# Moving the branch to the general path behind the first expert's gate products, with three experts in fixed places instead of two

## The chip, the cores and the metric

The kernel runs on one core of a Trainium2 chip. The metric is the device time of one execution in microseconds, lower is better; the medians below are of several executions. TensorE (PE), VectorE (DVE), ScalarE (ACT), GpSimd (POOL) and SyncE (SP) each work through a queue of their own in order, and wait for each other by semaphores.

## What is computed

Two decoder layers over 512 tokens of width 1024. Layer 0 mixes tokens by retention and a state-space scan, layer 1 by dilated attention; each layer then ends in a mixture of experts: every token goes to two of 16 SwiGLU experts, chosen by a router. Cut to what matters here:

```
logits -> best of 4 groups -> best 2 of its 4 experts, weights by softmax over the two
for each expert e, on the tokens sent to it:
    y = (silu(x @ w_gate[e]) * (x @ w_up[e])) @ w_down[e]      # 1024 -> 512 -> 1024
h = h + sum over the two experts of weight * y
```

A matrix of an expert is 2 MB in float32, so the 16 experts of a layer read 96 MB of weights.

## The kernel before

**The steps of the experts.** The 16 experts run one after the other in places that are heavy (128 rows) or light (64 rows), by the string STEPS = "HHHLHHLHLHHLHHLL". Experts 0 and 1 have fixed places. The other 14 are sorted by load, so that the seven fullest get the heavy places; `by_load` works out the order from the counts of tokens (DVE L1054 to L1058, then a small product on PE, L1060, that gives the list of expert numbers `ids`). If some expert has more rows than the plan holds, a general path (`moe_any`) must run instead. One number, `cmax`, tells this (DVE L1043): every engine loads it into a register (TENSOR_LOAD, L1410) and takes or skips the block (COMPARE_AND_BRANCH, L1411). With the inputs used here the block is skipped. Behind the skip each engine waits for its own earlier work, SP for every DMA it has issued, and the work of other engines from behind the branch waits for DVE to have passed it.

**A heavy step.** A 128-row product runs as three products of rounded parts (`mm3`, L197 to L199): each 128x1024 piece of a weight is split into a rounded part by ACT (CAST, L194) and a rest by DVE (TENSOR_TENSOR, L194), and six products follow for one piece, 24 for a matrix of four pieces. Two rest splits, one in expert 0's w_up and one in expert 1's w_gate, run on POOL. `gate(0)`, `proj(0, "w_up")` (called up(0) below), `gate(1)`, `down(0)` and up(1) follow in this order on PE. `gather(e)` brings an expert's rows into place: for expert 0 by products with a selection (L1249, L1254; one half of them needs token rows that POOL gathered from DRAM, L929), for the others by transposes of rows that `fetch(e)` gathered (POOL L1222). `listed(e)` works out the row numbers for it (PE L1024, L1025, DVE L1012, L1017, L1027). `weights` works out the weight of each row: exponentials on ACT (L1086, with a load of its table before and another after), a chain of small DVE operations (L1088 to L1097), a transpose and a product with the sorted order on PE (L190 on `wt`, L1104).

**The loads.** SP issues the loads of weights in program order, 1 MB each (L1190); where a matrix belongs to a sorted expert, its address needs `ids`, which SP reads by 14 register loads (L1420) behind the branch. F and R are rings of 1 MB buffers; a load waits until the last reader of its buffer is done.

**Order.** A scheduler in the kernel's framework lays each engine's instructions out by priority; `tc.issue_after` adds an order. The branch is a fence: no instruction crosses it.

Of the kernel before, what the change touches and what calls it, by code (L numbers as in the profile page):

```python
# [12 lines left out]
F32R = mybir.dt.float32r  # L13
# [25 lines left out]

STEPS = "HHHLHHLHLHHLHHLL"  # L40
NS = NE - 2
NHEAVY = STEPS[2:].count("H")
# [4 lines left out]
def _constants():  # L47
# [12 lines left out]
    e2 = np.arange(2, 16)  # L60
    th = np.where(e2[None, :] < e_[:, None], -0.5, 0.5)
    heavy, light = iter(range(NHEAVY)), iter(range(NHEAVY, NS))
    rank = [next(heavy) if k == "H" else next(light) for k in STEPS[2:]]
    blk = np.full((128, 4, NS), -1.0)
    for i in range(64):
        if i % 16 >= 2:
            blk[i, i // 16] = rank
    own = (np.arange(16)[None, :] == e_[:, None]).astype(np.float32)
    srt = np.concatenate([blk.reshape(128, 56), own, th], 1).astype(np.float32)
# [26 lines left out]
def kernel(ctx: ExitStack, tc: tile.TileContext, I, out, *_):  # L96
# [686 lines left out]
    def layer1_mix(xT, first):  # L783
# [6 lines left out]
        for hf in range(2):  # L790
# [44 lines left out]
            if hf == 0:  # L835
                params = router_params(1, nc.sync)
# [34 lines left out]
    def router(l, wr, br, wrb):  # L871
# [9 lines left out]
        if l == 0:  # L881
            srts.append(sm.tile([128, 208], F32, bufs=1, name="srt"))
            nc.scalar.dma_start(srts[0][:, 0:86], I["srt"])
# [88 lines left out]
        def chosen_of(c, pl, s0, s1):  # L972
# [9 lines left out]
            for i in range(2):  # L982
                sl = slice(512 * i, 512 * i + 512)

                a, b, o = h[:, c, sl], grow[:, sl], xn[:, sl].rearrange("q (k p) -> q p k", k=4)
                a, b = (t.rearrange("q (p k) -> q p k", k=4) for t in (a, b))
                scaled.append(V.scalar_tensor_tensor(o, a, rs, b, op0=OP.mult, op1=OP.mult))
                nc.scalar.dma_start(xnd[c * 128:(c + 1) * 128, sl], xn[:, sl])
            V.scalar_tensor_tensor(lg[:, c, :], pl, rs, br, op0=OP.mult, op1=OP.add)
            ranks(c)  # L990

        return chunk, q

    def route(q):
# [40 lines left out]
        def loads():  # L1035
# [4 lines left out]
            V.tensor_scalar(m14, pp[:, 4, 2:NE], LIGHT + 0.5, CAP / NHEAVY, op0=OP.is_gt, op1=OP.mult)  # L1040
# [9 lines left out]
        def by_load(bT):  # L1050

            cnt, rank, own, gt = srt[0:64, 116:117], srt[0:64, 117:118], srt[0:64, 86:102], srt[0:64, 120:134]
            P = srt[0:64, 134:190]
            V.tensor_tensor(own, srt[0:64, 56:72], pp[0:64, 4, :], op=OP.mult)  # L1054
            V.tensor_reduce(cnt, own, AX.X, OP.add)
            V.scalar_tensor_tensor(gt, pp[0:64, 4, 2:NE], cnt, srt[0:64, 72:86], op0=OP.subtract, op1=OP.is_gt)
            V.tensor_reduce(rank, gt, AX.X, OP.add)
            V.tensor_scalar(P, srt[0:64, 0:56], rank, None, op0=OP.is_equal)  # L1058
# [6 lines left out]
            V.tensor_copy(pos[:, :, 2:NE], pm)  # L1065
            return P, ids

        def weights(P=None, fits=None):
# [29 lines left out]
            if P is not None:  # L1098
# [6 lines left out]
                V.tensor_copy(wt[:, :, 2:NE], pm)  # L1105
# [67 lines left out]
    def moe(l, rt, norm, done, then=None):  # L1173
# [52 lines left out]
        def gather(e):  # L1226
# [39 lines left out]
        def proj(e, w):  # L1266
# [153 lines left out]
        got, vals = nc.values_load_multi_w_load_instructions(  # L1420
            row[0:1, :], engines=(mybir.EngineType.SP,), min_val=0, max_val=NE - 1,
            skip_runtime_bounds_check_because="sums of one-hot rows: each is one of 2 to 15, or 0")
        ids.update(zip(range(2, NE), vals))
        ids[0] = got[-1]
        listed(2, range(2))
        fetch(2)
        m2r.set([4, 5])
        hs, silu = gate(0)
# [85 lines left out]
```

## Time and profile before

| | us |
|---|---|
| median of 3 runs | 1144.22 (1142.65 to 1145.25) |
| the profiled execution | 1145.4 |
| its span in the trace | 1143.6 |
| PE busy | 1050.0 (92% of the span) |
| DVE busy | 734.0 (64%) |
| ACT busy | 562.2 (49%) |
| POOL busy | 190.1 (17%) |

The profile gives one profiled execution. A busy engine there is not one at its peak; the granted clock of PE is given for stretches of time. "Idle before" names the idle time of an engine just ahead of an instruction and what ended it. Each layer passes the branch once, near 283 us in layer 0 and 833 us in layer 1.

### The profile page before, as it was taken

Reading aid. Unit: us, or ns where it says so; the run is one execution under the profiler, and the core shown is the slowest. Engines: PE = TensorE matmul, PEld = TensorE weight load, DVE = VectorE, ACT = ScalarE, POOL = GpSimd, SP = SyncE. Lnnn points to the kernel's source line nnn. Section 1 sums busy time; section 2 is a strip of 40 time slices with the busy share of each in tenths; the row PEclk is TensorE's granted clock in tenths of the full one; section 3 lists DMA queues with packets and bytes.
Section 4 is the critical chain, followed back from the end, with each engine's and each line's share of the span. In section 5 each row is a group of like instructions: output and inputs, shape, how many; then the busy total and the mean of one; then the engine's idle time right before and its main releaser. Section 6 shows DMA issues by size and latency. Waiting matters only on the chain. (4 is left out here: it accounts for less than half of the span.)

```text
span 1143.6 us, 15992 instructions
## 1 busy us (share of the span) xinstructions
PE 1050.0 (92%) x5951; PEld 762.0 (67%) x5951; DVE 734.0 (64%) x1265; ACT 562.2 (49%) x852; POOL 190.1 (17%) x120
## 2 busy tenths in 40 slices
PE   5979899998799999989889999999978999999994
PEld 4766677786576765757368777877756676565641
DVE  6988952777797755756372273275679785565634
ACT  5433134524576644655353353354366675464634
POOL 3734110000312221221000000000012132211111
PEclk9999999999999999999989999999999999989998
DMA  7262323356699999999842315226349999999963
GB/s 239 74 147 104 101 78 111 107 216 240 240 381 380 380 380 383 373 374 374 309 179 75 110 37 184 74 75 234 141 170 396 354 382 392 388 385 377 367 243 147
DMA packets 84712, 277.38 MB, mean 243 GB/s; under 512 B 23714, under 2 KB 23898, under 8 KB 68368
## 3 DMA queue, kind: packets, MB, share of 16 engines
q1 hardware_dynamic: 72000, 248.31, 57.7%
q0 software_dynamic: 8016, 16.88, 5.9%
q10 hardware_dynamic: 4608, 11.06, 2.6%
q8 instruction: 51, 0.84, 0.3%
q14 instruction: 37, 0.30, 0.1%
HBM read 262.49 MB, written 24.12 MB: 251 GB/s over the span
## 5 line engine op out<-in xcount | busy, mean ns | idle before, releaser
L198 PE MATMUL acc<-R,R 128*128 128x512 f32 x936 | 381.1, 407 | 17.1 <-DVE R L194 16.3
L197 PE MATMUL acc<-R,R 128*128 128x512 f32 x860 | 350.9, 409 | 26.3 <-ACT R L194 16.5
L199 PE MATMUL acc<-R,R 128*128 128x512 f32 x860 | 342.8, 401 | 1.3 <-DVE R L194 1.3
L194 DVE TENSOR_TENSOR R<-F,R 128x1024 fp32r<-128x1024 f32 (+1 forms) x178 | 212.9, 1218 | 138.1 <-ACT R L194 133.1
L194 ACT CAST R<-F 128x1024 fp32r<-128x1024 f32 (+1 forms) x178 | 182.4, 1040 | 180.6 <-PE acc L199 107.7
L198 PEld LDWEIGHTS acc<-R,R 128*128 128x128 f32 x936 | 179.2, 191 | 67.7 <-DVE R L194 28.9
L197 PEld LDWEIGHTS acc<-R,R 128*128 128x128 f32 x860 | 164.2, 191 | 67.7 <-ACT R L194 22.5
L199 PEld LDWEIGHTS acc<-R,R 128*128 128x128 f32 x860 | 164.8, 192 | 37.7 <-DVE R L194 3.3
L1222 POOL DMA_INDIRECT F<-xnd,idx x30 | 50.9, 1698 | 238.7 <-DVE ws L1032 113.9
L1304 PE MATMUL acc<-F,R 128*64 128x512 f32 x304 | 71.2, 595 | 0.0
L194 DVE TENSOR_TENSOR R<-pb,R 128x512 fp32r<-128x512 f32 x84 | 57.3, 702 | 14.6 <-ACT R L194 14.5
L1376 POOL DMA_INDIRECT hd<-m,idx x20 | 36.6, 1829 | 147.8 <-ACT m L1375 146.0
L194 ACT CAST R<-pb 128x512 fp32r<-128x512 f32 x84 | 47.5, 586 | 27.4 <-PE pb L190 20.9
L194 DVE TENSOR_TENSOR R<-R,R 128x1024 fp32r<-128x1024 f32 x40 | 48.2, 1221 | 6.4 <-ACT R L194 6.0
L922 POOL MEMSET R<- 128x1024 f32 x2 | 1.9, 954 | 300.6 <-PE acc L199 300.6
L1304 PEld LDWEIGHTS acc<-F,R 128*64 128x64 f32 x304 | 22.0, 137 | 43.6 <-issue 43.2
L194 ACT CAST R<-R 128x1024 fp32r<-128x1024 f32 x40 | 41.4, 1050 | 13.2 <-PE acc L199 12.1
L197 PE MATMUL acc<-spare,R 128*128 128x512 f32 x116 | 45.7, 394 | 0.0
L199 PE MATMUL acc<-spare,R 128*128 128x512 f32 x116 | 45.7, 394 | 0.0
L190 PE MATMUL pb<-C,F 128*128 128x128 f32 (+1 forms) x296 | 37.5, 261 | 3.4 <-POOL F L490 3.4
L190 PE MATMUL pb<-C,m 128*128 128x128 f32 (+1 forms) x163 | 27.7, 292 | 12.7 <-DVE m L227 9.6
L1307 ACT ACTIVATE m2w<-acc 64x512 f32<-64x512 f32 x8 | 4.7, 593 | 68.5 <-PE acc L1304 68.5
(384 smaller groups left out, 1447.0 us busy)
## 6 DMA issues: line engine op xcount, KB each, us to landing
F<-in_moe_w_up_dram SPq DMA_DIRECT2D x46, 1024.0 KB, 22.4
F<-in_moe_w_down_dram SPq DMA_DIRECT2D x40, 1024.0 KB, 22.2
F<-in_moe_w_gate_dram SPq DMA_DIRECT2D x38, 1024.0 KB, 23.0
R<-in_moe_w_gate_dram SPq DMA_DIRECT2D x20, 1024.0 KB, 15.9
R<-in_moe_w_down_dram SPq DMA_DIRECT2D x12, 1024.0 KB, 24.9
h<-in_moe_w_down_dram SPq DMA_DIRECT2D x12, 1024.0 KB, 22.5
F<-in_c_w_qkv_dram SPq DMA_DIRECT2D x12, 1024.0 KB, 6.1
F<-in_ab_w_in_dram SPq DMA_DIRECT2D x10, 1024.0 KB, 5.1
```

Of the source, the lines that this page charges most:

```text
L190: PE.transpose(dst, src, ident[:n, :n])
L194: return S.copy(hi, src), eng.tensor_tensor(lo, src, hi.bitcast(F32), op=OP.subtract)
L197: PE.matmul(ps, ah, bh, start=first, stop=False)
L198: PE.matmul(ps, ah, bl, start=False, stop=False)
L199: return PE.matmul(ps, al, bh, start=False, stop=last)
L922: G.memset(q.x0, 0.0)
L1222: rows[e] = G.indirect_dma_start(out=xg[e % 2][0:n], out_offset=None, in_=xnd[:, :], in_offset=bass.IndirectOffsetOnAxis(ap=idx[0:n, e, 0: ...
L1304: m = PE.matmul(ps[LIGHT * i:LIGHT * i + LIGHT], x_[:, 4 * kk + k, :], raw[i][:, k, :], start=kk + k == 0, stop=kk + k == 4, skip_group_ch ...
L1307: silu = S.activation(hs[0:LIGHT], ps[LIGHT:2 * LIGHT], AF.Silu)
L1376: G.indirect_dma_start(out=hd[:, :], out_offset=bass.IndirectOffsetOnAxis(ap=idx[:, e, 1:2], axis=0), in_=y[:, :], in_offset=None, bounds_ ...
```

## The change

- FIXED = 3: experts 0, 1 and 2 have fixed places and 13 are sorted. The loads of expert 2's w_gate and of expert 1's w_down, 4 MB, stand ahead of the branch on SP, expert 2's w_up directly behind it, ahead of the register loads of `ids`.
- `by_load` and `gate(0)` stand ahead of the branch; so do three rest splits of up(0) (two on DVE, one on POOL). `listed` and `fetch` of experts 1 and 2 stand behind it. Expert 0's splits are ordered behind the sort's last DVE step.
- The router's parameters of layer 1 are loaded from layer 1's first mixing stage, no longer ahead of layer 0's branch. In the last 128 tokens of the router the logits and ranks stand ahead of the scaled rows.

The core of the diff (sizes of the table of the sort follow from 14 to 13 and are left out):

```diff
+FIXED = 3
-NS = NE - 2
-NHEAVY = STEPS[2:].count("H")
+NS = NE - FIXED
+NHEAVY = STEPS[FIXED:].count("H")
...
-                params = router_params(1, nc.sync)
+                with tc.issue_after(fr.load.ins):
+                    params = router_params(1, nc.sync)
...
+            if c < 3:
+                rows()
             V.scalar_tensor_tensor(lg[:, c, :], pl, rs, br, op0=OP.mult, op1=OP.add)
             ranks(c)
+            if c == 3:
+                rows()
...
-            V.tensor_scalar(P, srt[0:64, 0:56], rank, None, op0=OP.is_equal)
+            by_load.last = V.tensor_scalar(P, srt[0:64, 0:4 * NS], rank, None, op0=OP.is_equal)
...
-            if e < 2:
+            if e < FIXED:
                 return wv[w][e, r0:r1, :].rearrange(f"{rows} n -> p k n", p=128)
...
-            with tc.issue_after(ids[0].ins) if (e, w) == (1, "w_down") else nullcontext():
-                fr.load = nc.sync.dma_start(t, rows_of(e, w, r0, r1))
+            fr.load = nc.sync.dma_start(t, rows_of(e, w, r0, r1))
...
-                with after(loads.last.ins) if e == 0 else nullcontext():
+                with after(by_load.last.ins) if e == 0 else nullcontext():
...
-                    for i in (rt.last, rt.sqrt) + (gather.last if k2 else ()) if held else ():
+                    for i in (rt.last, rt.sqrt, by_load.last) + (gather.last if k2 else ()) if held else ():
...
         cf, bT = loads()
+        perm, row = by_load(bT)
         gather(0)
+        table(AF.Silu)
+        R[wrs[2]] = typed(wrs[2:], F32R)[0]
+        m2r.set([4, 5])
+        hs, silu = gate(0)
         top = nc.values_load(cmax[0:1, 0:1], min_val=0, max_val=T)
+        m2r.set([0, 1])
+        m4r.set([0, 1])
         with tc.If(top > CAP):
             moe_any(l, weights(), xg[1])
-        table(AF.Silu)
+        m2r.set([5, 4])
         m4r.set([1])
-        R[wrs[2]] = typed(wrs[2:], F32R)[0]
-        perm, row = by_load(bT)
         listed(1, range(2))
         fetch(1)
         listed(0, range(2), rt.oh)
-        got, vals = nc.values_load_multi_w_load_instructions(
+        _, vals = nc.values_load_multi_w_load_instructions(
...
         listed(2, range(2))
         fetch(2)
-        m2r.set([4, 5])
-        hs, silu = gate(0)
```

The line numbers in the rows of the changed kernel are some 4 to 15 higher than before (L194 becomes L198, L197 to L199 become L201 to L203). In the rows of the order R_, F_ and m_ are buffers with their numbers.

On DVE in layer 0, about the branch, before: R_84, R_85 are expert 0's w_gate pieces, R_82 its rows.

```order
L194 TENSOR_TENSOR R_84<-R_2390,R_84 128x1024
L1043 CAST cmax<-cf 128x1
L194 TENSOR_TENSOR R_82<-acc,R_82 128x512 x2
L1056 SCALAR_TENSOR_TENSOR srt<-pb,srt 64x14
L194 TENSOR_TENSOR R_85<-R_2390,R_85 128x1024
L1410 TENSOR_LOAD cmax
L1411 COMPARE_AND_BRANCH
```

The same place in the changed kernel; R_2390 and R_2391 hold w_gate, F_70 the first half of w_up.

```order
L198 TENSOR_TENSOR R_84<-R_2390,R_84 128x1024
L198 TENSOR_TENSOR R_85<-R_2390,R_85 128x1024
L198 TENSOR_TENSOR R_2444<-R_2391,R_2444 128x1024
L1443 TENSOR_SCALAR cf<-cf 128x1
L198 TENSOR_TENSOR R_84<-R_2391,R_84 128x1024
L198 TENSOR_TENSOR R_85<-F_70,R_85 128x1024
L198 TENSOR_TENSOR R_2444<-F_70,R_2444 128x1024
L1425 TENSOR_LOAD cmax
L1428 COMPARE_AND_BRANCH
```

All four rest splits of gate(0) and two of up(0) now precede DVE's branch; before, two of gate(0) did and the sort was cut in two by it.

On PE in layer 0, the end of up(0) before; `wt` is the table of the rows' weights, F_79 the rows that were fetched for expert 1, `spare` the rounded part whose rest POOL splits.

```order
L197 MATMUL acc<-R_84,R_82 128x512
L198 MATMUL acc<-R_84,R_82 128x512
L190 MATMUL pb<-C,wt 64x128
L199 MATMUL acc<-R_84,R_82 128x512
L197 MATMUL acc<-spare_2874,R_82 128x512
L198 MATMUL acc<-R_2873,R_82 128x512
L199 MATMUL acc<-spare_2874,R_82 128x512
L197 MATMUL acc<-spare_2874,R_82 128x512
L1104 MATMUL pb<-srt,m_1_91 128x56
L190 MATMUL pb<-C,F_79 128x128 x8
```

The same place in the changed kernel:

```order
L201 MATMUL acc<-spare_2872,R_82 128x512
L202 MATMUL acc<-R_2871,R_82 128x512
L203 MATMUL acc<-spare_2872,R_82 128x512
L201 MATMUL acc<-spare_2872,R_82 128x512
L202 MATMUL acc<-R_2871,R_82 128x512
L203 MATMUL acc<-spare_2872,R_82 128x512
L194 MATMUL pb<-C,wt 64x128
L1115 MATMUL pb<-srt,m_1_91 128x52
L194 MATMUL pb<-C,F_79 128x128 x8
```

The transpose of `wt` stood within up(0), with seven of its products still behind it (five are in the rows, two stand behind expert 1's transposes), and now stands behind up(0)'s last product.

On SP in layer 0 the loads that led up to the branch in the changed kernel (before, the row of F_76 was the last of the weights here):

```order
L1200 DMA F_77<-in_moe_w_down_dram 128x2x1024
L1200 DMA F_76<-in_moe_w_up_dram 128x2048
L1200 DMA R_2389<-in_moe_w_down_dram 128x2x1024
L1200 DMA R_2387<-in_moe_w_gate_dram 128x2048
L1200 DMA R_2388<-in_moe_w_down_dram 128x2x1024
L1425 TENSOR_LOAD cmax
L1425 ISA x2
L1428 COMPARE_AND_BRANCH
```

R_2389, R_2387, R_2388 are loads that stood behind the branch and behind `ids`; F_78, likewise, now stands earlier still.

## Rows read from the trace of the kernel before

**Rows 1.** PE's timeline (start, us, engine, line, operation, tiles, idle before) in both layers

```profile
288.08 0.77 PE L197 MATMUL acc<-R,R 128*128 128x512 f32 x1 [4.58 <-DVE srt L1058]
...
312.85 0.50 PE L198 MATMUL acc<-R,R 128*128 128x512 f32 x1 [2.32 <-DVE R L194]
...
316.85 0.50 PE L197 MATMUL acc<-R,R 128*128 128x512 f32 x1 [0.73 <-ACT R L194]
...
830.36 2.05 PE L1254 MATMUL acc<-m,F 128*128 128x128 f32 x16
836.90 0.47 PE L197 MATMUL acc<-R,R 128*128 128x512 f32 x1 [4.50 <-DVE srt L1058]
...
848.71 0.50 PE L198 MATMUL acc<-R,R 128*128 128x512 f32 x1 [2.62 <-DVE R L194]
...
855.91 0.39 PE L197 MATMUL acc<-R,R 128*128 128x512 f32 x1
856.14 0.40 PE L198 MATMUL acc<-R,R 128*128 128x512 f32 x1
...
861.65 0.80 PE L198 MATMUL acc<-R,R 128*128 128x512 f32 x1 [2.35 <-DVE R L194]
...
862.67 0.63 PE L197 MATMUL acc<-R,R 128*128 128x512 f32 x1
863.10 0.63 PE L198 MATMUL acc<-R,R 128*128 128x512 f32 x1
...
867.12 0.50 PE L197 MATMUL acc<-R,R 128*128 128x512 f32 x1 [0.72 <-ACT R L194]
```

**Rows 2.** Sequencer records of the branch, line L1411, both layers (ns min/median/max)

```profile
L1411 PEldq COMPARE_BRANCH  x2: 3328/3378/3427, 284.4 to 833.2; - x2
```

**Rows 3.** DVE's timeline in layer 1

```profile
831.43 1.21 DVE L194 TENSOR_TENSOR R<-R,R 128x1024 fp32r<-128x1024 f32 x1
...
832.63 1.27 DVE L194 TENSOR_TENSOR R<-acc,R 128x512 fp32r<-128x512 f32 x2
...
842.56 0.68 DVE L1012 TENSOR_TENSOR m2w<-C,pos 128x512 bf16<-128x512 f32 x1
...
844.50 2.90 DVE L1017 TENSOR_TENSOR junk<-C,pos 128x512 bf16<-128x512 f32 x1
...
850.92 0.16 DVE L1088 TENSOR_REDUCE gv<-gd 128x4 f32<-128x16 f32 x1
...
852.13 0.23 DVE L1097 TENSOR_TENSOR wt<-wt,m 128x64 f32<-128x64 f32 x1
```

**Rows 4.** POOL's timeline in layer 1

```profile
844.47 2.38 POOL L194 TENSOR_TENSOR R<-F,spare 128x1024 fp32r<-128x1024 f32 x1 [0.29 <-DVE idx L1027]
```

**Rows 5.** ACT's timeline in layer 1

```profile
845.97 0.60 ACT L1297 ACTIVATE m<-acc 128x512 f32<-128x512 f32 x1 [0.62 <-PE acc L199]
846.46 1.04 ACT L194 CAST R<-F 128x1024 fp32r<-128x1024 f32 x1
847.51 1.28 ACT L1086 ACT_TABLE_LOAD   x1
```

**Rows 6.** Windows of layer 1: busy time by engine, granted clock, DMA share, GB/s

```profile
845.00:850.00 5.00, 2.38 (x11) 1.64 (x10) 5.00 (x6) 4.33 (x6) 3.13 (x2) 1.00 0.87 314
...
860.00:870.00 10.00, 7.62 (x28) 6.02 (x29) 7.74 (x9) 3.96 (x6) 2.25 (x2) 0.83 1.02 388
```

**Rows 7.** ACT's waits, 318 to 572 us (us in total, times, longest)

```profile
ACT R L194 <- DMA F<-in_moe_w_up_dram: 0.9, 1, 0.9
```

**Rows 8.** POOL's timeline in layer 0, first token rows gathered

```profile
270.60 1.80 POOL L929 DMA_INDIRECT R<-xnd,idx  x1 [29.37 <-DVE rs L219]
```

**Rows 9.** Landing times of the gathers of line L929

```profile
DMA to landing us min/median/max: 4.2/4.7/5.1
```

**Rows 10.** PE's timeline in layer 0 about that gather

```profile
273.20 0.40 PE L199 MATMUL acc<-R,R 128*128 128x512 f32 x1
...
276.96 2.03 PE L1249 MATMUL acc<-C,R 128*128 128x128 f32 x16
```

More of the change, by code (lines that the diff above doesn't have):

```diff
@@ L59, in _constants @@
     e_ = p % 16
-    e2 = np.arange(2, 16)
+    e2 = np.arange(FIXED, NE)
     th = np.where(e2[None, :] < e_[:, None], -0.5, 0.5)
     heavy, light = iter(range(NHEAVY)), iter(range(NHEAVY, NS))
-    rank = [next(heavy) if k == "H" else next(light) for k in STEPS[2:]]
+    rank = [next(heavy) if k == "H" else next(light) for k in STEPS[FIXED:]]
     blk = np.full((128, 4, NS), -1.0)
     for i in range(64):
-        if i % 16 >= 2:
+        if i % 16 >= FIXED:
             blk[i, i // 16] = rank
     own = (np.arange(16)[None, :] == e_[:, None]).astype(np.float32)
-    srt = np.concatenate([blk.reshape(128, 56), own, th], 1).astype(np.float32)
+    srt = np.concatenate([blk.reshape(128, 4 * NS), own, th], 1).astype(np.float32)
     cst[:, C_EC] = e_
@@ L882, in router @@
             srts.append(sm.tile([128, 208], F32, bufs=1, name="srt"))
-            nc.scalar.dma_start(srts[0][:, 0:86], I["srt"])
+            nc.scalar.dma_start(srts[0][:, 0:S_TAB], I["srt"])
         q.srt = srts[0]
@@ L981, in chosen_of, with rows @@
                 q.xn.append(xn)
[L982 to L988, printed above, removed]
+            def rows():
+                for i in range(2):
+                    sl = slice(512 * i, 512 * i + 512)
+                    a, b, o = h[:, c, sl], grow[:, sl], xn[:, sl].rearrange("q (k p) -> q p k", k=4)
+                    a, b = (t.rearrange("q (p k) -> q p k", k=4) for t in (a, b))
+                    scaled.append(V.scalar_tensor_tensor(o, a, rs, b, op0=OP.mult, op1=OP.mult))
+                    nc.scalar.dma_start(xnd[c * 128:(c + 1) * 128, sl], xn[:, sl])
+            if c < 3:
+                rows()
             V.scalar_tensor_tensor(lg[:, c, :], pl, rs, br, op0=OP.mult, op1=OP.add)
             ranks(c)
+            if c == 3:
+                rows()
         return chunk, q
@@ L1050, in by_load @@
         def by_load(bT):
-            cnt, rank, own, gt = srt[0:64, 116:117], srt[0:64, 117:118], srt[0:64, 86:102], srt[0:64, 120:134]
-            P = srt[0:64, 134:190]
-            V.tensor_tensor(own, srt[0:64, 56:72], pp[0:64, 4, :], op=OP.mult)
+            cnt, rank, own, gt = srt[0:64, 116:117], srt[0:64, 117:118], srt[0:64, 86:102], srt[0:64, 120:120 + NS]
+            P = srt[0:64, 134:134 + 4 * NS]
+            V.tensor_tensor(own, srt[0:64, S_OWN:S_TH], pp[0:64, 4, :], op=OP.mult)
             V.tensor_reduce(cnt, own, AX.X, OP.add)
-            V.scalar_tensor_tensor(gt, pp[0:64, 4, 2:NE], cnt, srt[0:64, 72:86], op0=OP.subtract, op1=OP.is_gt)
+            V.scalar_tensor_tensor(gt, pp[0:64, 4, FIXED:NE], cnt, srt[0:64, S_TH:S_TAB], op0=OP.subtract, op1=OP.is_gt)
             V.tensor_reduce(rank, gt, AX.X, OP.add)
-            V.tensor_scalar(P, srt[0:64, 0:56], rank, None, op0=OP.is_equal)
+            by_load.last = V.tensor_scalar(P, srt[0:64, 0:4 * NS], rank, None, op0=OP.is_equal)
             pi = bank(shape=(1, NS))
@@ L1064, in by_load @@
             PE.matmul(pm.rearrange("p c s -> p (c s)"), bT, P, start=True, stop=True)
-            V.tensor_copy(pos[:, :, 2:NE], pm)
+            V.tensor_copy(pos[:, :, FIXED:NE], pm)
             return P, ids
@@ L1419, in moe @@
         listed(0, range(2), rt.oh)
-        got, vals = nc.values_load_multi_w_load_instructions(
+        _, vals = nc.values_load_multi_w_load_instructions(
             row[0:1, :], engines=(mybir.EngineType.SP,), min_val=0, max_val=NE - 1,
-            skip_runtime_bounds_check_because="sums of one-hot rows: each is one of 2 to 15, or 0")
-        ids.update(zip(range(2, NE), vals))
-        ids[0] = got[-1]
+            skip_runtime_bounds_check_because="sums of one-hot rows: each is one of FIXED to 15, or 0")
+        ids.update(zip(range(FIXED, NE), vals))
         listed(2, range(2))
         fetch(2)
-        m2r.set([4, 5])
-        hs, silu = gate(0)
         fr.set([[0, 2, 3, 4, 7, 5, 6, 1, 8, 12, 13, 14, 10, 11], [1, 3, 4, 2, 6, 0, 7, 5, 8, 12, 13, 14, 10, 11]][l])
```

5 lines of the change are left out of this document (3 added, 2 removed).

## The prediction

> **What bounds the kernel now.** I read first the busy time of the engines: PE 92% of the span, no other above 64%. So what counts is where PE stands still, and the timeline of PE with its idle times shows that next. At the change's place it stands still three times in each layer [rows 1]: 4.50 us (4.58 in layer 0) from the end of expert 0's gather to the first gate product, 2.62 us at the start of up(0), 2.35 us (2.32) in the middle of gate(1). The reader is to see the releaser of each: the first is put down to DVE's sort (L1058), the others to a rest split. Then the records of the branch itself: on PE's sequencer the jump over the block takes 3.33 and 3.43 us [rows 2]. So the first gap has two causes of nearly one length, the jump and DVE's queue (rest splits and sort), which run side by side. The two other gaps come from POOL: its split takes 2.38 us from 844.47 [rows 4], and a DVE operation that starts 0.03 us later takes 2.90 us [rows 3], where the operation of the same size ahead of it took 0.68. DVE does next to nothing while POOL splits.
>
> That is how the trace shows it, and the page "Trainium Architecture — The Big Picture" of the Trainium skill, section "What this means for kernel authors", gives the rule: DVE and GpSimd contend for one port pair, and it is an exclusive lock, not a split of bandwidth. The trace agrees, with 2.90 beside 2.38 us. Were it a split, a POOL split beside DVE would cost about half, and each sum below would be some 1.2 us lower per layer.
>
> Last the windows: from 845 to 850 the DMA engines are 87% busy [rows 6], and PE waits for no load; ACT waits for one load in all of layer 0's expert steps, 0.9 us [rows 7].
>
> **The change part by part.** Times are those of layer 1 in the profiled execution. The four parts are gate(0), the branch, the weights and gate(1); then the loads.
>
> *Gate(0) ahead of the branch.* Expert 0's gather ends on PE at 830.36 + 2.05 = 832.41 [rows 1]. In the new order of DVE, an operation of 0.68 us that waits for this end, and the sort's last step (0.24, an estimate by its class: it is smaller), come first: 833.35. Then two splits of the rows (1.27 for both) and some 0.3 of small casts: 834.95. Rest splits follow at 1.21 each [rows 3]: 836.2, 837.4, 838.6. The fourth reuses the buffer of the first, so it needs the first's six products (6 x 0.23 = 1.4, by the distance of 855.91 and 856.14 [rows 1]), then an ACT cast of 1.04 [rows 5]: 838.65, so 839.9. Its six products end at 841.3. Before, the gate's end was read by ACT at 845.97 [rows 5]: 4.7 us gained.
>
> *The branch behind it.* PE's jump costs its 3.4 us wherever it stands, and at its new place PE has nothing to run beside it: 841.3 + 0.3 for the register + 3.4 = 845.0. DVE comes to the same time: POOL's split starts when the fourth rest split is done, 839.9, and holds DVE until 842.3; two rest splits of up(0) make it 844.7, and PE's first work behind the branch waits for DVE to have passed. So of 4.7 us about 3.7 come back as a new idle time between gate(0) and up(0). In exchange the 2.62 us at 848.71 are gone, since POOL's split and its two followers lie under the jump. After some 24 small products of `listed` (0.7 us, an estimate from their start distances), up(0) begins at 845.8 and runs 24 x 0.23 = 5.6 us, to 851.4. Were the jump to go, PE would still wait for DVE's 844.7; only with both away does the gain stay.
>
> *The weights behind up(0).* ACT now has two casts that wait for up(0)'s own products (1.04 each, the second can start at 848.7 and ends at 849.8), then the load of the exponentials' table, 1.28, and the exponentials: 851.3. On DVE the product with up(0)'s result is ahead of the rest of the chain, then nine small operations, 850.92 to 852.36 or 1.4 us [rows 3]: 853.6. PE, which had the transpose of `wt` within up(0), now has nothing between 851.4 and 853.6: a new wait of 2.2 us. Its cover before was seven products of up(0); that is gone.
>
> *Gate(1).* The product with the sort's order and the transposes of expert 1's rows take about 1.6 us: 855.2. POOL's second split starts about then, as soon as ACT has cast its input, and DVE cannot split expert 1's rows before 857.7; with 0.64 us for a first half gate(1) starts at 858.4 and runs 5.6 us, to 864.0. The 2.35 us gap in it is gone, since the wait now lies ahead of it. By the distance from the last row at half speed to 867.12, down(0) starts 1.4 us later: 865.4, 1.7 us before the row's 867.12 [rows 1]. Layer 0 had 316.85 - 288.08 = 28.8 us from restart to down(0), layer 1 30.2 [rows 1]; what differs is the half-speed stretch at 861.65. So in layer 0 the same sum gives only 0.3 us. Both: -2.0.
>
> *The clock.* After the idle 4.50 us PE runs at half speed, in both layers; after 2.35 us it did in layer 1 and did not in layer 0 (0.63 us long rows, 0.43 apart, against 0.50 at 312.85 [rows 1]; granted clock 0.83 over 860 to 870 [rows 6]). At half speed PE has 1.2 of its 2.4 GHz. A mean of 0.83 over 10 us is 3.4 us at half; that holds 8 products at 0.43 instead of 0.23, so it costs 1.6 us where PE sets the pace. Before, the first stretch lay in gate(0), where splits set much of the pace. Now the idle times are 2.5 us ahead of gate(0), 3.7 ahead of up(0), and 2.2 and 2.9 ahead of gate(1). Nothing of this length but 4.50 and 2.35 is in the rows, so the bounds are no stretch (0) and two on the path in each layer (+6.4); 3.7 lies nearer to 4.50, so I take one in each layer: +3.1, rounded with its partial overlap of `listed`.
>
> *The loads.* 4 MB of weights go out ahead of the branch, and 2 MB more before SP reads `ids`. In layer 1 the DMA engines are nearly idle there, and nothing on the path waits for them: 0. In layer 0 two of these loads find their buffers free only when products up to 273.20 + 0.40 have read them [rows 10], while the gather of expert 0's rows (issued at 270.60 [rows 8], 4.2 to 5.1 us to land [rows 9], so 275.7) is in flight; its reader starts at 276.96 [rows 10], 1.2 us of room. If the last 2.1 us of the gather run at half rate it lands at 277.8: +0.9, which I take. If it had to wait for both megabytes at 388 GB/s (2.1 MB, 5.4 us), it would land at 279 or later: about +2. If nothing is shared: 0. Behind the branch the stream of loads is some 11 us ahead (4 x 1.05 MB at 388 GB/s); there is one wait for a load of 0.9 us to win [rows 7], of which I take 0.6.
>
> *The rest at nothing.* The parameters of layer 1's router move on SP alone, and are a few kilobytes each. The logits ahead of the rows for the last tokens move DVE's work under products of L1249 and L1254, which PE runs ahead of the counts anyway. One sorted place fewer shortens DVE operations of 0.2 us by nothing that shows.
>
> **Sum:** -2.0 + 3.1 + 0.9 - 0.6 = +1.4 us on 1145.4. The profiled execution is 1.2 us above the median, so 1145.7 against 1144.22.
>
> **The rivals.**
>
> *The gain at up(0) is kept.* up(0) starts 2.6 to 2.9 us earlier in each layer. For it to last, the weights' chain would have to be hidden (if ACT's casts come sooner than I have them) and no half-speed stretch fall on the path. Then -2.6 twice, and -1.4 for layer 1's stretch at 861.65: 1138 or so; with only the second, -2.0 - 0.6 = 1141.6. Middle: 1140. For it speaks that 2.35 and 2.62 us left the clock alone in two of the rows; against it that PE's program has the transpose of `wt` behind all of up(0).
>
> *The jump goes.* If PE's sequencer gets past the branch while PE still works on queued products, and DVE with it, 3.4 us more per layer go: about 1136. Against it: the jump took 3.3 to 3.4 us both times [rows 2], and DVE is not there before 844.7.
>
> *Slower: the clock.* More pauses in place of one long one mean more stretches at half speed, and now on up(0) and gate(1), whose 5.6 us are all PE's. With two in each layer: -2.0 + 6.4 + 0.9 - 0.6 = +4.7, and up to +1 more from the gather: 1149 to 1150.2. It decides from the third of the four stretches on (-1.7 + 3 x 1.6 = +3.1, over the bound). For it speaks the row at 861.65, where 2.35 us were enough; against it 312.85.
>
> **How the numbers follow.** A measurement of this kernel tells about 0.2%, 2.3 us, from no change: 1141.9 to 1146.5 is the same. My forecast, 1145.7 (1143 to 1148), has a chance of 0.42 (0.03 faster, 0.33 same, 0.06 slower); the gain kept, 0.26 (0.22 faster, 0.04 same); the jump gone, 0.05, faster; the clock, 0.27 (0.24 slower, 0.03 same). So faster 0.30, same 0.40, slower 0.30. The range from 1139 to 1150.5 leaves out the jump's case, the far end of the kept gain and the far end of the clock's.
>
> **What would show it.** Right: PE's gap ahead of gate(0) down to 2 to 3 us, a new one of 3 to 4 us ahead of up(0) that ends with DVE or with PE's own sequencer, one of about 2 us ahead of the transpose of `wt`, one ahead of gate(1) that ends with a rest split beside POOL's; down(0) 28 to 30 us behind the first product's old place. Wrong: PE's branch record well under 3 us; no gap ahead of `wt`; in layer 0 the products of L1249 more than 1 us late, with an idle time ahead of them that ends with a DMA. The forecast falls if stretches at half speed number none or four, or if a part far from the branch moves by more than a microsecond.

## The result, and the profile after

| | before | after |
|---|---|---|
| median, us | 1143.45 (1142.65 to 1145.25, 4 runs) | 1132.81 (1130.76 to 1133.92, 4 runs) |
| ratio, 95% interval | | 0.9903 (0.9881 to 0.9924) |
| span of the profiled execution, us | 1143.6 | 1132.1 |

The change is 1% faster, some 11 us. The prediction said 1145.7 with a range from 1139: it was 13 us too high, and the time lies below its range.

At the branch the trace shows much of what was predicted. PE's timeline of the changed kernel, first layer 0, then layer 1 (the rows answer to those of [rows 1]):

```profile
285.87 0.50 PE L202 MATMUL acc<-R,R 128*128 128x512 f32 x1 [2.03 <-DVE R L198]
294.50 0.18 PE L1035 MATMUL pb<-tl,junk 128*128 128x2 bf16 x1 [3.05 <-DVEq L1428]
304.04 0.30 PE L194 MATMUL pb<-C,wt 128*64 128x128 f32 x1 [1.80 <-DVE wt L1108]
...
831.76 0.50 PE L202 MATMUL acc<-R,R 128*128 128x512 f32 x1 [2.03 <-DVE R L198]
840.37 0.18 PE L1035 MATMUL pb<-tl,junk 128*128 128x2 bf16 x1 [3.06 <-DVEq L1428]
842.56 0.16 PE L1036 MATMUL pb<-rc,m2w 128*128 128x2 bf16 x1 [1.55 <-issue]
852.63 0.30 PE L194 MATMUL pb<-C,wt 128*64 128x128 f32 x1 [1.92 <-DVE wt L1108]
853.28 0.42 PE L1115 MATMUL pb<-srt,m 64*128 64x52 f32 x2 [0.35 <-ACT m L1113]
857.39 0.79 PE L203 MATMUL acc<-R,R 128*128 128x512 f32 x1 [1.18 <-DVE R L198]
```

The gap of 4.5 us ahead of gate(0) is down to 2.0. A new one of 3.1 us stands behind gate(0) and ends with DVE's sequencer at the branch. The weights' chain, hidden before, now holds PE for 1.9 + 0.35 us, and a rest split that stands behind POOL's second one (854.26 to 856.62 us) holds gate(1). All four were steps of the prediction. So the gain must have come from elsewhere.

Three views show where. First the costliest groups of the page (line, operation, shapes, count, busy us, mean ns, idle before and its releaser), before and then after. They are the first two products of `mm3`, L197 and L198 before; the third, L199, waits for 1.3 us before:

```profile
L198 PE MATMUL acc<-R,R 128*128 128x512 f32 x936 | 381.1, 407 | 17.1 <-DVE R L194 16.3
L197 PE MATMUL acc<-R,R 128*128 128x512 f32 x860 | 350.9, 409 | 26.3 <-ACT R L194 16.5
```

```profile
L202 PE MATMUL acc<-R,R 128*128 128x512 f32 x936 | 378.0, 404 | 6.5 <-DVE R L198 6.5
L201 PE MATMUL acc<-R,R 128*128 128x512 f32 x860 | 351.8, 410 | 7.6 <-ACT R L198 6.6
```

PE's idle time ahead of them is down from 43.4 to 14.1 us. That is far more than the gaps at the branch hold.

Second, the distance between the light gates, which are blocks of 32 products that stand in the same order in every kernel. The start of each block in PE's timeline (before: 428.72, 484.39, 539.15; after: 428.84, 478.10, 529.01) gives:

| start of light gate to the next, us | before, layer 0 | after, layer 0 | before, layer 1 | after, layer 1 |
|---|---|---|---|---|
| expert 3 to 6 | 49.2 | 49.2 | 49.0 | 49.0 |
| 6 to 8 | 30.7 | 31.0 | 30.5 | 30.9 |
| 8 to 11 | 55.7 | 49.3 | 57.1 | 49.0 |
| 11 to 14 | 54.8 | 50.9 | 56.2 | 50.9 |

The gain lies in the two late stretches: 10.3 us in layer 0 and 13.4 in layer 1, 23.7 together, more than 100 us behind the branch. What the changed kernel loses elsewhere brings this down to 11.

Third, what PE waited for in the first of these stretches before. PE's timeline, then ACT's:

```profile
438.08 0.50 PE L197 MATMUL acc<-R,R 128*128 128x512 f32 x1 [0.63 <-ACT R L194]
439.03 0.50 PE L197 MATMUL acc<-R,R 128*128 128x512 f32 x1 [0.44 <-ACT R L194]
...
457.95 0.50 PE L197 MATMUL acc<-R,R 128*128 128x512 f32 x1 [1.55 <-ACT R L194]
459.21 0.80 PE L198 MATMUL acc<-R,R 128*128 128x512 f32 x1 [0.76 <-DVE R L194]
```

```profile
435.88 0.59 ACT L1307 ACTIVATE m2w<-acc 64x512 f32<-64x512 f32 x1 [12.10 <-PE acc L1304]
436.50 0.58 ACT L194 CAST R<-pb 128x512 fp32r<-128x512 f32 x1
436.98 1.05 ACT L194 CAST R<-F 128x1024 fp32r<-128x1024 f32 x1
```

ACT stands idle for 12.1 us until the light gate of expert 8 is done, for its silu (L1307) is next in its queue; the casts of w_down of expert 7 come behind it, and PE then waits for them. The same four waits come again at 493.75 to 514.74, and in layer 1. They are 3.4 of the 6.4 us by which the first stretch of layer 0 is longer than in the changed kernel. The rest is slower products behind them, part of it at half speed (the granted clock over the stretch is 0.97, and 1.00 in the changed kernel). After, ACT has these casts ahead of the silu, with the loads just in time:

```profile
428.46 1.05 ACT L198 CAST R<-F 128x1024 fp32r<-128x1024 f32 x1 [1.22 <-DMA F<-in_moe_w_down_dram]
429.41 1.04 ACT L198 CAST spare<-F 128x1024 fp32r<-128x1024 f32 x1
436.00 0.59 ACT L1317 ACTIVATE m2w<-acc 64x512 f32<-64x512 f32 x1 [5.55 <-PE acc L1314]
```

Two things have changed there at once. The scheduler has put the casts ahead of the silu; and the loads are in fact earlier. The experiments are to tell these apart, and to price the branch by itself. (One correction to what stands ahead: the branch is not a fence for everything. Loads that depend on nothing behind it are issued ahead of it, and so the early loads are possible.)

### The profile page after: what moved, and what is told of

Its sections match the earlier page's. It is cut to its first block, busy times and chain, and to the rows that moved or that the text cites. A ratio compares the mean times of both kernels' runs of the same rounds, so it can differ in the third digit from the quotient of the medians.

```text
span 1132.1 us, 15979 instructions
## 1 busy us (share of the span) xinstructions
PE 1051.2 (93%) x5951; PEld 769.5 (68%) x5951; DVE 731.5 (65%) x1265; ACT 569.7 (50%) x856; POOL 187.2 (17%) x120
## 5 line engine op out<-in xcount | busy, mean ns | idle before, releaser
L201 PE MATMUL acc<-R,R 128*128 128x512 f32 x860 | 351.8, 410 | 7.6 <-ACT R L198 6.6
L203 PE MATMUL acc<-R,R 128*128 128x512 f32 x860 | 342.3, 401 | 3.5 <-DVE R L198 3.5
L198 DVE TENSOR_TENSOR R<-F,R 128x1024 fp32r<-128x1024 f32 (+1 forms) x178 | 217.0, 1236 | 166.7 <-ACT R L198 161.1
L198 ACT CAST R<-F 128x1024 fp32r<-128x1024 f32 (+1 forms) x178 | 182.5, 1040 | 208.1 <-PE acc L203 117.3
L201 PEld LDWEIGHTS acc<-R,R 128*128 128x128 f32 x860 | 164.8, 192 | 51.5 <-ACT R L198 12.7
L203 PEld LDWEIGHTS acc<-R,R 128*128 128x128 f32 x860 | 165.0, 192 | 42.1 <-DVE R L198 6.0
L1232 POOL DMA_INDIRECT F<-xnd,idx x30 | 48.0, 1600 | 226.8 <-DVE ws L1043 151.0
L198 DVE TENSOR_TENSOR R<-pb,R 128x512 fp32r<-128x512 f32 x84 | 56.5, 686 | 13.1 <-ACT R L198 12.7
L198 ACT CAST R<-pb 128x512 fp32r<-128x512 f32 x84 | 47.8, 587 | 30.1 <-PE pb L194 24.4
L198 DVE TENSOR_TENSOR R<-R,R 128x1024 fp32r<-128x1024 f32 x40 | 47.6, 1220 | 6.9 <-ACT R L198 6.7
L198 ACT CAST R<-R 128x1024 fp32r<-128x1024 f32 x40 | 41.5, 1050 | 12.5 <-PE acc L203 12.3
L203 PE MATMUL acc<-spare,R 128*128 128x512 f32 x116 | 45.6, 393 | 0.0
L201 PE MATMUL acc<-spare,R 128*128 128x512 f32 x116 | 45.4, 392 | 0.0
L194 PE MATMUL pb<-C,F 128*128 128x128 f32 (+1 forms) x296 | 41.2, 274 | 3.4 <-POOL F L494 3.4
L194 PE MATMUL pb<-C,m 128*128 128x128 f32 (+1 forms) x163 | 26.5, 285 | 17.2 <-DVE m L231 14.2
L194 PEld LDWEIGHTS pb<-C,m 128*128 128x128 f32 (+1 forms) x163 | 19.4, 146 | 30.2 <-issue 11.6
```

The source lines that it names most:

```text
L194: PE.transpose(dst, src, ident[:n, :n])
L198: return S.copy(hi, src), eng.tensor_tensor(lo, src, hi.bitcast(F32), op=OP.subtract)
L201: PE.matmul(ps, ah, bh, start=first, stop=False)
L203: return PE.matmul(ps, al, bh, start=False, stop=last)
L1232: rows[e] = G.indirect_dma_start(out=xg[e % 2][0:n], out_offset=None, in_=xnd[:, :], in_offset=bass.IndirectOffsetOnAxis(ap=idx[0:n, e, 0: ...
```

## The experiments

Ratios are to the kernel before, on the same chip; one percent is 11.4 us. The kernel before has medians from 1143.5 to 1148.8 us on the chips used, so kernels are compared by ratio. Where times of stretches are given "by the starts of like instructions", they come from one profiled execution each.

| run | edit | ratio (95% interval) | light gates 8 to 11, 11 to 14, layer 0 | layer 1 |
|---|---|---|---|---|
| before | | 1 | 55.7, 54.8 | 57.1, 56.2 |
| after | | 0.9903 (0.9881 to 0.9924) | 49.3, 50.9 | 49.0, 50.9 |
| e1 | branch at its old place | 0.9829 (0.9793 to 0.9865) | 49.3, 50.6 | 49.0, 50.4 |
| e2 | changed kernel with two fixed | 1.0046 (1.0025 to 1.0067) | 49.5, 57.6 | 49.3, 58.2 |
| e3 | before, other order alone | 0.9919 (0.9893 to 0.9945) | 52.1, 52.1 | 52.0, 52.3 |
| e4 | 4 MB copied behind the branch | 0.9988 (0.9965 to 1.0012) | 49.3, 51.0 | 49.0, 50.8 |
| e5 | table load held | 0.9877 (0.9847 to 0.9908) | 49.3, 50.5 | 49.0, 50.5 |
| e6 | e1, no split on POOL | 0.9789 (0.9756 to 0.9822) | 49.3, 50.5 | 49.0, 50.5 |
| e7 | e1, two gathers held | 0.9824 (0.9795 to 0.9853) | 50.2, 49.9 | 50.1, 49.8 |
| e8 | before, three fixed and early loads alone | 0.9816 (0.9787 to 0.9845) | 49.3, 50.5 | 49.1, 50.4 |
| e9 | before, fast order forced, no lead | 0.9924 (0.9897 to 0.9951) | 50.8, 53.0 | 50.6, 56.4 |
| e10 | e8, old order forced, lead kept | 0.9838 (0.9812 to 0.9864) | 51.0, 51.0 | 50.9, 50.8 |
| e11 | e8, loads held | 0.9964 (0.9946 to 0.9982) | 55.9, 54.8 | 55.8, 56.0 |
| e12 | e8, no split on POOL | 0.9758 (0.9734 to 0.9782) | 49.3, 50.5 | 49.0, 50.5 |

Some results fit none of what was expected: e2 (1151.3 us) is slower than both of its theories, and the medians of e3 (1137.7), e5 (1131.3) and e10 (1128.8) lie between the ranges of two theories.

### The two halves of the change: e1, e2 and e8

e1 is the changed kernel with `by_load`, `gate(0)` and the rest of the tail where the kernel before has them.

```diff
-        perm, row = by_load(bT)
         gather(0)
-        table(AF.Silu)
...
-        hs, silu = gate(0)
         top = nc.values_load(cmax[0:1, 0:1], min_val=0, max_val=T)
...
         with tc.If(top > CAP):
             moe_any(l, weights(), xg[1])
...
+        table(AF.Silu)
...
+        perm, row = by_load(bT)
...
+        hs, silu = gate(0)
```

> The changed kernel with its branch, sort and gate(0) back at the old place; three fixed experts, the early loads, the router's parameters and the order of the last rows stay. Theory O: the gain comes late in the experts' steps (about -10 us in layer 0 from 420 to 530 us, -13 in layer 1 from 970 to 1075), where a new order of PE closes waits of 0.6 + 0.4 + 1.6 + 0.8 us in two places per layer; the order there is that of the changed kernel, so this gain stays, and the +1.1 and +2.3 us that the new branch cost at the start of the steps are gone: 1126 to 1131. Theory S: the gain comes from the branch behind the gate products: 1142 to 1145.

e2 is the changed kernel with its branch behind gate(0), but two fixed experts, so that none of expert 2's loads can go ahead. Expert 1's w_down, 2 MB, still goes ahead of the branch (SP issues it from 263.63 us).

```diff
-FIXED = 3
+FIXED = 2
```

> The changed kernel with FIXED = 2: 14 experts are sorted, expert 2's 4 MB cannot be loaded ahead of the branch; branch, sort and gate(0) stay moved. Theory O: of the two places in each layer whose waits closed, the first keeps the new order and the second has the old one again, so about half of the late gain is lost (4 to 6 us per layer): 1139 to 1144. Theory S: 1132 to 1134, as the branch is still moved.

e8 is e1 without the edits of the router's parameters and rows: the kernel before with three fixed experts and their loads, and nothing else.

```diff
-                with tc.issue_after(fr.load.ins):
-                    params = router_params(1, nc.sync)
+                params = router_params(1, nc.sync)
...
-            if c < 3:
-                rows()
+            rows()
```

> The kernel before with three fixed experts and their early loads alone: the router's parameters and the last rows stand where they stood before. The order on PE, row for row, is that of e1_branch_early. If these two edits are worth nothing: as e1, 1124 to 1128. If not, the difference is theirs.

The third fixed expert with its early loads gains 1.84% (21 us). e1 and e8 differ by less than their intervals, so the smaller edits are worth nothing that shows. In the changed kernel the moved branch takes part of the 21 back: e1 stands 0.74% (8.5 us) ahead of it. e2, 0.46% (5 us) slower than the kernel before, is no price of the move alone. By the starts of like instructions it gains 9.2 us in the late stretches (its row in the table) and loses 5.6 us at the branch of layer 0, 6.6 at that of layer 1 and 4.1 in layer 1's mixing; PE's jump, 6.4 us in it, and the mixing are taken up below.

### Order or lead: e3, e7, e9, e10, e11

e3 leaves loads and branch as before and calls `gather(e + 2)` ahead of `down(e)` for experts 8 and 11.

```diff
-            if e + 1 < NE:
+            if e + 1 < NE and e not in (9, 12):
                 gather(e + 1)
...
+            if e in (8, 11):
+                gather(e + 2)
```

> The kernel before, with one edit: for the steps 8 and 11 (light ones between two heavy ones) the rows of the expert after next are gathered ahead of the light step's down products, not behind. Loads, branch and sort as before. Theory O with order alone: the waits of 1.55 + 0.76 us and the half-speed stretch after one of them in each layer go at both places, about 2.3 to 4 us each, 1130 to 1135. Theory L (the lead of the loads is what pays, or is needed): the loads are no earlier than before, and in the kernel before some of them land only a few us ahead of their use, so PE waits for loads instead: 1140 to 1144.

e7 is e1 with the transposes of experts 10 and 13 held behind the light steps' down products, close to their old place.

```diff
+                        with after(pe[-1].ins) if e in (10, 13) else nullcontext():
+                            tr(pts[i][:, a, :], x_[:, blk])
```

> The kernel of e1_branch_early, with the order of the kernel before put back at one kind of place: the rows for experts 10 and 13 are transposed behind the down products of the light steps 8 and 11, two places per layer; loads and their lead as in e1. Theory O (the order pays): the waits of 1.55 + 0.76 us come back at each place, and where the clock falls some 1.6 us more, 9 to 16 us in all: 1134 to 1141. Theory L (the lead pays): 1125 to 1128.

e3 gains 0.8% by order alone, so order can matter; e7 shows that these two gathers are not what it hangs on. What differs between the queues is ACT's: the casts ahead of the silu or behind it. So the last set forces just that. e9 is the kernel before with the order of the fast kernels: in `down(7)` and `down(10)` the casts (four and two) come first, then the silu of the light gate, then the rest, and the transposes of gather(9) and gather(12) stand behind the down products.

```diff
+            ahead = [wsplit(raw[i // 2][:, :, i % 2 * 512:i % 2 * 512 + 512]) for i in range({7: 4, 10: 2}.get(e, 0))]
+            with ExitStack() as st:
+                if ahead:
+                    with after(wsplit.hi.ins):
+                        st.enter_context(after(silu().ins))
+                evac = split_to(hh, hl, pt)
...
+                        with after(pe[-1].ins) if e in (9, 12) else nullcontext():
+                            tr(pts[i][:, a, :], x_[:, blk])
```

> The kernel before, with two fixed experts and its loads as they were, but with the order of the fast kernels forced at two places of each layer: ScalarE casts w_down of experts 7 and 10 (four and two tiles) ahead of the silu of the light step that follows, instead of behind it, and the transposes of gather(9) and gather(12) stand behind the down products of experts 7 and 10. Theory order (the early loads only made the scheduler choose this order, and the order is the whole gain): 1122 to 1127 us, and the waits of PE on ScalarE's casts near 438, 458, 494 and 513 us are gone. Theory lead (4 MB loaded ahead of the branch are the gain, since the DMA engines are full from 350 us to the end of the layer): 1141 to 1146, the casts now wait for their loads instead. If both are needed: 1130 to 1139.

e10 is e8 with the opposite: the casts of `down(7)` and `down(10)` held behind that silu, the loads early.

```diff
-                        for i in evac if k2 >= 1 and e >= 8 else ():
+                        for i in (evac if k2 >= 1 and e >= 8 else ()) + ((silu,) if e in (7, 10) else ()):
```

> Experiment e8 (three fixed experts and their early loads alone, 1124.5) with ScalarE's casts of w_down of experts 7 and 10 held behind the silu of the light step that follows, as they stand in the kernel before; the loads keep their lead. Theory order: 1140 to 1146, with PE's waits on ScalarE's casts back, some 5 us at each of four places. Theory lead: 1122 to 1127. If both are needed: 1130 to 1139.

e11 is e8 with the early loads held until SP has read `ids`, as before.

```diff
+            with tc.issue_after(ids[0].ins) if (e, w) in ((1, "w_down"), (2, "w_gate")) else nullcontext():
+                fr.load = nc.sync.dma_start(t, rows_of(e, w, r0, r1))
...
+                with tc.issue_after(ids[0].ins):
+                    for k2 in range(2):
```

> Experiment e8 with the loads of expert 2 and the last load of expert 1 held on SP's queue until the sorted list is read, as the kernel before has them: three fixed places, thirteen sorted, no lead. The scheduler falls back to the order of the kernel before in both late places. Both theories: 1141 to 1147, within 0.3% of the kernel before. A time under 1135 would say that neither loads nor order make the gain, but the third fixed place itself.

Without the early loads the third fixed place gains little: e11 has the four waits of the kernel before to within 0.01 us, and gains 0.36%. e8 and e11 differ only in whether the loads of experts 1 and 2 are held, and by 1.48% (17 us). So the early loads are the cause. Whether they pay by arriving earlier or by the order that the scheduler chooses with them is a second question. With them, the old order of those casts costs only 0.2% (e10 against e8, less than their intervals). Without them, the forced order gains 0.76% of 1.84% (e9).

How much of the lead is left at the late stretches can be read from the bytes moved. Windows from one and the same product (L738, at 208.04 before) to the start of the light gate of expert 6, in the kernel before, the changed kernel, e2 and e8 (the second number is the length, the last GB/s):

```profile
208.04:398.01 189.97, 176.52 (x1014) 135.91 (x1012) 148.75 (x293) 103.81 (x148) 32.29 (x19) 0.99 0.78 288
205.07:397.82 192.75, 180.33 (x1014) 139.86 (x1012) 151.79 (x296) 104.91 (x147) 30.79 (x19) 0.96 0.78 291
203.72:399.43 195.71, 180.72 (x1015) 140.01 (x1013) 151.56 (x296) 104.87 (x146) 30.16 (x19) 0.96 0.75 280
205.53:395.64 190.11, 176.49 (x1014) 135.87 (x1012) 151.81 (x296) 104.94 (x148) 29.43 (x19) 0.99 0.82 298
```

Length times rate gives 54.7, 56.1, 54.8 and 56.7 MB. So of 4 MB the changed kernel is here still 1.4 MB ahead, some 3.6 us at 388 GB/s, e8 1.9 MB, and e2 has no lead at all. Yet in its first late stretch e2 has the casts ahead of the silu and none of PE's four waits, and takes 49.5 and 49.3 us, as the kernels with a lead do. ACT's timeline of e2:

```profile
431.25 1.99 ACT L198 CAST R<-F 128x1024 fp32r<-128x1024 f32 x2 [5.74 <-DVE m2w L1455]
437.60 0.59 ACT L1317 ACTIVATE m2w<-acc 64x512 f32<-64x512 f32 x1 [1.81 <-PE acc L1314]
```

From light gate 8 to 11, then, the order alone can bring the whole gain, and e9's forced order (50.8) is not quite the order of the fast kernels. From 11 to 14, e2 has the old order and its four waits (57.6). There no run has the fast order without a lead: the order of e3 brings part (52.1), that of e9 part in layer 0 (53.0) and nothing in layer 1, the lead with the old casts brings 51.0, and both together 50.5. ACT's timeline of e9 shows what its order lacks, at the place of the second silu:

```profile
487.56 1.99 ACT L194 CAST R<-F 128x1024 fp32r<-128x1024 f32 x2 [9.91 <-DMA F<-in_moe_w_down_dram]
```

The casts stand ahead of the silu as in the fast kernels, and wait 9.9 us for their load. In e8 the same wait is 2.4 us, at 474.66. And in e10, with the lead, PE's first pair of waits is back (438.65 here), but the pair of 1.55 and 0.76 us is not:

```profile
438.65 0.50 PE L201 MATMUL acc<-R,R 128*128 128x512 f32 x1 [0.63 <-ACT R L198]
439.60 0.51 PE L201 MATMUL acc<-R,R 128*128 128x512 f32 x1 [0.44 <-ACT R L198]
```

e10 does not show that the lead closed that second pair: in e9, without a lead, it is gone too.

Windows of the kernel before (the last two numbers are the DMA share and GB/s) show that a missing lead is hard to make up:

```profile
430.00:440.00 10.00, 8.93 (x53) 4.29 (x50) 3.43 (x6) 4.09 (x7) 1.86 (x1) 1.00 1.04 398
450.00:460.00 10.00, 7.69 (x44) 3.98 (x43) 4.61 (x8) 5.39 (x8) 2.13 (x2) 0.94 1.00 372
```

From 350 to 540 us the DMA share is 0.91 or more, at 340 to 420 GB/s in most windows, and a load into F lands 22 to 23 us after its issue (medians of the profile's page). But the lead is not the whole of it: at light gate 14 the changed kernel has moved some 1.6 MB less than the kernel before (106.3 against 107.9 MB by the same sum), so by this estimate its late stretches are shorter in part because it uses loads sooner after they land.

What stays open: e10 and e9 change the order at two places of each layer only, and the scheduler places other casts by the early loads too. How the gain divides between lead and order from 11 to 14 is not separated.

### A lead that could not be taken away: e4

e4 copies 4 MB from DRAM to DRAM on SP's queue behind the reading of `ids`, to use up the lead of the changed kernel.

```diff
+        for kk in range(4):
+            with tc.issue_after(got[-1].ins):
+                nc.sync.dma_start(junkd[512 * kk:512 * kk + 512, :], wv["w_gate"][kk // 2, 512 * (kk % 2):512 * (kk % 2) + 512, :])
```

> The changed kernel with 4 MB of copies from DRAM to DRAM put into SP's queue behind the reading of the experts' numbers, so that the stream of loads loses its lead of some 11 us; the order on PE, DVE and ACT is that of the changed kernel, row for row. Theory O with order alone: 1133 to 1135. Theory L: PE waits for loads in the late steps, and 5 to 11 us per layer come back: 1140 to 1150.

It is 1 us from the kernel before, as the theory of the lead wanted, but for another reason. The late stretches kept their gain (49.3 and 51.0 us). The loss came at the branches: by the starts of like instructions e4 loses 9.8 us from 250 to 320 us and 7.2 from 820 to 880, the changed kernel 2.8 and 2.3. PE's record of the jump, in the changed kernel, in e2 and in e4 (ns, least, median, most):

```profile
L1428 PEldq COMPARE_BRANCH  x2: 3312/3490/3668, 290.3 to 836.1; - x2
```

```profile
L1428 PEldq COMPARE_BRANCH  x2: 6368/6400/6432, 288.2 to 844.7; - x2
```

```profile
L1429 PEldq COMPARE_BRANCH  x2: 8228/8340/8452, 290.8 to 842.7; - x2
```

So e4 tells nothing of the lead; it tells of the jump (below).

### The small losses of the changed kernel: e5, e6, e12

e5 holds the load of ACT's table for the first silu behind the router's last square root.

```diff
-        table(AF.Silu)
+        with after(rt.sqrt.ins):
+            table(AF.Silu)
```

> The changed kernel with one order added: the load of ACT's silu table waits for the router's last square root. In the changed kernel nothing holds it, since it no longer stands behind the branch, and it was laid out in layer 1's first mixing stage, where ACT then loads a table again in the middle of the norm (1.28 us) and PE waits 2.7 us. If this is where the +3.7 us of that stage come from: 1128 to 1131. If the stage is slower for another reason (the branch's move changes the order there too): 1132 to 1134.

In the changed kernel this load is no longer kept back by the branch, and the scheduler moved it up; the mixing of layer 1 then has to load its own table in the middle of its norm. ACT's and PE's timelines of the changed kernel:

```profile
572.61 1.28 ACT L222 ACT_TABLE_LOAD   x1
```

```profile
577.18 1.72 PE L194 MATMUL pb<-C,m 128*128 128x128 f32 x8 [2.73 <-DVE m L231]
```

By the starts of like instructions, from 574 to 654 us of the kernel before, the changed kernel loses 3.7 us, e2 and e4, which do not hold this load either, 4.1 and 4.0, and e5 nothing. So the cause of this loss is shown. The time as a whole does not tell e5 from the changed kernel (0.9877 against 0.9903, intervals that overlap).

e6 is e1, and e12 is e8, with POOL's two splits given to DVE.

```diff
-        pool = [(0, "w_up", 3), (1, "w_gate", 3)]
+        pool = []
```

> The kernel of e1_branch_early (branch at the old place, three fixed experts) with the two rest splits of each layer that POOL ran given to DVE. If DVE stands still while POOL splits (2.4 us each), the waits ahead of up(0) and in gate(1), 3.4 and 0.7 to 1.1 us per layer, shrink by half or more, since DVE needs 1.22 us for such a split itself: 1120 to 1124. If DVE is short of time there anyway: 1125 to 1128.

> Experiment e8 (three fixed experts and their early loads, the branch where the kernel before has it) with the two splits of GpSimd given to VectorE, which gained 1 to 3 us in e6. Every theory: 1119 to 1124, faster than the changed kernel by 9 to 14 us.

Each stands ahead of its base, by 0.40% and by 0.58%; the first pair's intervals overlap, the second pair's do not. In the traces the wait ahead of up(0) in layer 0 falls from 3.44 us (e1, e8) to 0.57 (e6, e12). That POOL's split stops DVE shows in the changed kernel too, first POOL's, then DVE's timeline:

```profile
835.66 2.38 POOL L198 TENSOR_TENSOR R<-F,spare 128x1024 fp32r<-128x1024 f32 x1 [8.69 <-DVE R L198]
```

```profile
835.68 4.58 DVE L198 TENSOR_TENSOR R<-F,R 128x1024 fp32r<-128x1024 f32 x2
```

Two rest splits that take 1.2 us each last 4.58. e12 (1120.76 us, ratio 0.9758) is the best kernel here: it beats the changed kernel, 0.9903, by 1.5%, and leaves the branch where it was.

## Why the prediction was wrong

- **The loads: the step that failed.** It said that "there is one wait for a load of 0.9 us to win [rows 7]" and took -0.6 us. The loads gained 17 us (e8 against e11), 21 with the third fixed place. The step looked only at waits that end with a DMA. The waits that mattered end with a cast of ACT, and the casts came late because they stood behind a silu in ACT's queue. The early loads changed that order. The lead of 11 us, which the prediction computed and gave no value, is down to some 3.6 us at the light gate of expert 6. The step also counted one wait too few, for ACT has a second one in the same stretch, of 0.59 us:

```profile
397.96 1.04 ACT L194 CAST R<-F 128x1024 fp32r<-128x1024 f32 x1 [0.59 <-DMA F<-in_moe_w_down_dram]
```

- **What changed far away was not looked at.** The prediction followed the new order from the gather to down(0). The queues of PE, ACT and DVE differ again some 130 us on, at experts 7 to 12. The sentence that the forecast falls "if a part far from the branch moves by more than a microsecond" named what to look for.
- **Gate(0) and the branch: right.** 3.7 us was expected as the new idle time behind gate(0); the rows give 3.05 and 3.06, and 1.55 more in layer 1. The jump took 3.3 to 3.7 us, as [rows 2].
- **The weights: right.** 2.2 us expected; 1.80 + 0.42 and 1.92 + 0.35 measured.
- **Gate(1): right in kind.** Its wait beside POOL's second split is 1.2 us in layer 1 and 0.3 in layer 0, less than the 2.9 assumed, and it lies within gate(1), not ahead of it.
- **The clock: taken too low.** One stretch at half speed on the path was taken for each layer. In the profiled execution there are two behind gate(0) in each layer, one behind the pause of 3.1 us and one behind the waits of 1.8 to 1.9 and 0.4. Two in each layer were the condition of the rival "Slower: the clock". Windows of the changed kernel (the third number from the end is the granted clock):

```profile
294.60:298.00 3.40, 3.40 (x31) 2.82 (x31) 2.90 (x11) 0.00 (x0) 2.37 (x2) 0.50 0.62 189
304.80:311.60 6.80, 6.50 (x27) 5.04 (x28) 5.44 (x11) 2.61 (x4) 3.30 (x2) 0.50 1.01 425
840.70:847.50 6.80, 5.25 (x28) 4.16 (x26) 3.44 (x11) 1.04 (x1) 2.38 (x2) 0.50 0.92 283
854.40:861.20 6.80, 5.62 (x22) 4.07 (x21) 4.95 (x10) 2.14 (x3) 3.16 (x2) 0.50 1.00 418
```

- **The sum at the branch: right in sign, too small.** -2.0 + 3.1 + 0.9 gives +2.0 us for both layers. By the starts of like instructions the changed kernel loses 2.8 us from 250 to 320 and 2.3 from 820 to 880; the slower rival's -2.0 + 6.4 + 0.9 = +5.3 is nearer. But these are single executions, and the spread is as large: e9, whose program is here that of the kernel before, has four stretches at half speed too, and is 3.6 us longer than it in the first of these spans and 0.9 shorter in the second. The rival that the jump goes is dead. The forecast and all three rivals were about this part; a time in the range of the faster ones would have been luck.
- **Losses without a term:** the table's load in layer 1's mixing (3.7 us, shown by e5), and the ends of both layers, behind the last light gate but one (2.6 and 3.0 us). For the ends the cause is not shown. The stream of loads may set the pace there again, since the changed kernel lets it stand during the branch: its windows 280 to 300 show a DMA share of 0.11 and 0.43:

```profile
280.00:290.00 10.00, 7.15 (x43) 5.83 (x41) 8.92 (x23) 5.43 (x7) 0.52 (x2) 1.00 0.11 41
290.00:300.00 10.00, 6.95 (x46) 5.38 (x45) 8.18 (x14) 5.40 (x6) 4.87 (x3) 0.83 0.43 135
```

In e8, with the branch early, the same two have 0.43 and 0.94.

## What to carry to other kernels

Where the DMA engines are full for a long stretch, transfers that start earlier can be worth far more than the waits that end with a DMA: look at the DMA share by windows first, then ask of each wait on another engine what stood ahead of the awaited instruction in its queue, and why it was put there. If a scheduler lays the queues out, compare the order over the whole program, for here an early load moved instructions a hundred microseconds behind it. Count the bytes moved up to the place in question before calling a lead the cause. And measure the parts of a change alone: here one part gained 21 us, and the other took 8.5 of them back.

## What the runs showed of the hardware

- The jump over the same long block takes PE's sequencer longer where transfers run beside it. In the kernels before and after, and in e8, it took 3.3 to 3.7 us, with a DMA share of 0.03 to 0.46 during the jump; in e2 6.4 us, in e4 8.2 and 8.5. The windows of the jumps in e2 and in e4, whose last three numbers are the granted clock, the DMA share and GB/s:

```profile
288.20:294.60 6.40, 0.98 (x5) 0.47 (x3) 4.12 (x5) 3.50 (x4) 2.76 (x1) 0.89 0.87 330
844.70:851.10 6.40, 1.75 (x8) 1.11 (x6) 4.58 (x5) 3.96 (x5) 2.01 (x1) 0.88 0.74 308
```

```profile
290.80:299.00 8.20, 2.56 (x11) 1.72 (x10) 3.86 (x5) 4.42 (x5) 1.76 (x1) 0.92 0.78 267
842.70:851.10 8.40, 1.66 (x8) 1.01 (x6) 4.72 (x5) 3.86 (x4) 2.05 (x1) 0.77 0.85 292
```

The trace shows where the time goes. In the jumps of the kernels before and after, of e2 and of e4 one packet of 16 KB moves on queue q8, of the kind "instruction". It is first there in the DMA view of 290.3 to 291.4 us in the changed kernel, 288.2 to 292.2 in e2 and 290.8 to 296.5 in e4; in views shorter by 0.1 us it is not:

```profile
q8 instruction: 1, 0.02, 7.4%
q8 instruction: 1, 0.02, 1.5%
q8 instruction: 1, 0.02, 1.2%
```

So it starts some 1.0, 4.0 and 5.7 us into the jump of layer 0, and the jump ends about 2.5 us behind its start in all three: what grows is the wait for this packet to start. That the other transfers hold it up fits these kernels, but the DMA share alone does not order them (0.87 at 6.4 us, 0.78 at 8.2), and no run changed the transfers alone with the jump at a fixed place. The page "Runtime: NRT & Kernel Launch" of the Trainium skill, section "Instruction fetch mechanics", says that a taken branch whose target lies outside the fetched window forces a DMA fetch of the target. The packet on q8 agrees with that.
